# Reordering the row pairs of a hybrid decoder layer, splitting two embedding inputs at an earlier point, and scaling the last down-projection in PSUM

## The chip, the cores and the metric

The kernel runs on one core of a Trainium2 chip. The metric is device time in microseconds (us) of one execution; the median of several executions is compared. The engines are named as the profile names them: PE (TensorE, matmuls), PEld (its weight loads), DVE (VectorE), ACT (ScalarE), POOL (GpSimd) and SP (SyncE, which here issues nearly all DMA transfers). Each engine works through its own queue in order.

## The reference

One decoder layer over 1024 tokens with 1024 features, in float32. The parts that matter here, cut from the reference:

```python
h = x + mixed @ w_o                                # mixed: attention and convolution branches, normalised
a = rms_norm(h, ln_ffn_g) @ w_up                   # 1024 -> 2 x 2816
gate, up = split(a)
gate = causal_dwconv(gate, ffn_conv_w) + ffn_conv_b
h = h + (silu(gate) * up) @ w_down                 # 2816 -> 1024
h = h + sigmoid(rms_norm(h, ln_ple_g) @ w_pg) * (p_l @ w_pe)
```

`p_l` has 256 features per token: it is the embedding input, held transposed as `pT`.

## The kernel before

**Arithmetic.** Features lie on the 128 partitions and tokens along the free axis, in two halves of 512 (hf 0 and 1). Every float32 product is made of three matmuls: each operand is split into a high part (a cast to fp32r, `act.copy` or a POOL pass) and a low part (`dve.tensor_sub`, value minus high part), and `mm3` (L99 to L103) adds hi times hi (L101), hi times lo (L102) and lo times hi (L103). So each weight block and each activation costs, beside its load, one cast and one DVE subtraction before its matmuls.

**Row pairs (about 650 to 705 us).** The output projection `w_o` makes 8 row tiles per token half. Half 1 is done first in the loop at L944. Half 0 is done in four pairs (k, k+4) by `pair` (L1092), in between the first products of the up projection. For each row tile, `row` does 12 matmuls, and `row_rest` (L890) then does: DVE multiplies the PSUM tile by the token factor `rab` (L894), DVE adds the residual into `hm` (L896), SP writes `hm` to `hD`, ACT scales it into `y` (L899), ACT squares it (L903), DVE adds the square to `fssq` (L904). `forms_of` (L906) then makes the operands of a seven-product (Strassen-like) scheme out of four tiles of `y`: POOL makes t1, t2 and t4, DVE makes t3, and `keep_form` (L874) splits b22, t1, t3, t2 and t4 into a high part on ACT (L880) and a low part on DVE (L881). t3, t2 and t4 of pair k (the `late_` half of `forms_of`) are put one slot later, after the next pair's `row_rest`.

**What sets the order there.** This stage is written within a manual schedule (L1101): its loop goes over product slots n; each slot runs the matmuls of its pair or product, then the work that `behind(slot, delay, rank, function)` queued for it, sorted by rank, and `split(n + AHEAD)` puts the casts (`wbh`, L997) and subtractions (`wbl`, L998) of coming weight blocks in after the work of rank 0 and 1. POOL also makes sums of weight blocks (`wsum`, L984). In the lists below a tile named `bp` is a row tile in PSUM, `forms` is the tile that holds the split operands, `uv` is a copy of a product that ACT makes (L1058).

**Down projection (1110 to 1365 us).** The 22 gated activation tiles are taken in six groups of 3, 4, 4, 4, 4 and 3 (L1165). `act_parts` (L1134) loads and splits an activation (`acth`, `actl`). `down_group` (L1143) goes over 8 row tiles m: it loads and splits a block of `w_down` (`wraw`, `wh`, `wl`), does the matmuls of both token halves into PSUM tiles `ba`, and DVE adds them into `h` (L1154). In group 4 POOL then multiplies `h` by `rfb` and adds `hD` (L1160, L1163). In the last group DVE multiplies the PSUM tile by `rfb` into an SBUF tile `t` (L1157) and adds it to `h` (L1158).

**Embedding and gate (1358 to 1489 us).** `embed` (L1176) does the matmuls with `pT` and `w_pe`; two such tiles come before the gate projection, which needs all eight splits `fh`, `fl` (L1198, L1199) of the finished `h`. POOL adds six of the squares for the last norm (L1207).

**Order in this part.** Outside the manual schedule the framework orders each engine's queue by program order and readiness in its own model. `mark()` remembers the last instruction on every engine. A load with `after=` a mark gets a dependence on the mark's ACT instruction (L89 to L95), and the ACT cast in `weights` (L128) comes behind the mark in the queue. `pT` (two blocks of 512 KB) and `w_pe[0]` use the mark `last`. All `wraw` tiles share a ring of three buffers, and the DMAs are issued in order on SP.

Of the kernel before, what the change touches and what calls it, by code (L numbers as in the profile page):

```python
# [48 lines left out]
def _emit(nc, tc, d, out, tap=lambda *a: None):  # L49
# [824 lines left out]
    def keep_form(nm, k, y):  # L874
        i = FORMS.index(nm)
        where = i < 2, k
        if where not in forms_:
            forms_[where] = S([P, 2 if i < 2 else 5, 2, 512], F32R, f"forms{i < 2:d}{k}")
        hi, lo = (forms_[where][:, i if i < 2 else i - 2, z] for z in range(2))
        act.copy(hi, y)  # L880
        dve.tensor_sub(lo, y, f32(hi))  # L881
        form[nm][k] = hi, lo

# [6 lines left out]
    def row_rest(m, hf, ps):  # L890

        s = slice(hf * 512, (hf + 1) * 512)
        fs = fssq[:, s]
        dve.tensor_mul(ps, ps, rab[:, s])  # L894
        hm, g = S([P, 512], F32, "hm", 3), small["g_ffn"][:, m:m + 1]
        dve.tensor_add(hm, ps, hins[m, hf])  # L896
        nc.sync.dma_start(hD[m][:, s], hm)
# [1 line left out]
        act.activation(y, hm, AF.Copy, scale=g)  # L899
        if m == 0:  # L900
            act.square(fs, hm)
        else:
            act.square(ps, hm)  # L903
            dve.tensor_add(fs, ps, fs)  # L904

    def forms_of(k, late_=False):  # L906

        y11, y21, y12, y22 = (yf[m, hf] for hf in (1, 0) for m in (k, k + 4))

        def sub(nm, a, b, eng):  # L910
            z = yf[nm, k] = S([P, 512], F32, f"yt1{k}" if nm == "t1" else "yt", 1 if nm == "t1" else 3)
            eng.tensor_sub(z, a, b)
            return z
        if not late_:
            t1 = sub("t1", y12, y11, pool)
            keep_form("b22", k, y22)
            yf["t2", k] = sub("t2", y22, t1, pool)
            yf["t3", k] = sub("t3", y22, y12, dve)
            keep_form("t1", k, t1)
        else:  # L920
            z = sub("t4", y21, yf["t2", k], pool)
            for nm in ("t3", "t2"):
                keep_form(nm, k, yf[nm, k])
            keep_form("t4", k, z)
# [19 lines left out]
    for m in range(KC):  # L944
# [5 lines left out]
        row_rest(m, 1, ps)  # L950
        keep_form("b11" if m < 4 else "b21", m % 4, yf[m, 1])
# [140 lines left out]
    def pair(n, k):  # L1092
        tiles = [PS("bp", 4) for _ in range(2)]
        for m, ps in zip((k, k + 4), tiles):
            row(m, 0, ps)
# [89 lines left out]
    eh, el, wpe = [], [], {}  # L1185
    pT_h, pT_l = [], []
    for k in range(2):
        hi, lo = weights(d["pT"][k], 1024, tag="pT", bufs=2, after=last, by_act=True)
        pT_h.append(hi)
        pT_l.append(lo)  # L1190
# [147 lines left out]
```

## Time and profile before

| | us |
|---|---|
| median of 3 runs | 1489.8 |
| lowest and highest | 1489.61, 1490.05 |
| the profiled execution's own time | 1490.71 |
| its span in the trace | 1488.9 |
| PE busy within the span | 1433.8 |
| DVE busy | 990.5 |
| ACT busy | 584.2 |
| POOL busy | 492.6 |

The span runs from the first to the last instruction of the one execution that was profiled. PE is busy for 96% of it, so a saving is to be had only where PE stands idle or runs at the lower clock. In the trace's lists an idle time in square brackets stands just before an instruction, with the engine and line that released it. A duration of a matmul holds some overlap with the next; the distance between two starts is the true pace.

### The profile page before, as it was taken

What the parts mean: (1) busy time and instruction counts of PE and PEld (TensorE: products, weight loads), DVE (VectorE), ACT (ScalarE), POOL (GpSimd) and SP (SyncE); (2) the same over time, 40 slices, a digit from 0 to 9 for tenths busy, and PEclk for the clock granted to TensorE, in tenths of its full rate; (3) what the DMA queues carried; (4) which work ended last, traced back from release to release, by engine and by line L of the source; (5) the groups of instructions that cost most, each with busy time, mean ns of one, the idle gap of its engine ahead of it and who ended that gap; (6) DMA issues with size and microseconds to landing.
All of it is one profiled execution on the core that took longest, in us unless ns stands there. A gap on an engine that the chain in (4) does not pass through costs nothing.

```text
span 1488.9 us, 19441 instructions
## 1 busy us (share of the span) xinstructions
PE 1433.8 (96%) x7207; PEld 1168.9 (79%) x7207; DVE 990.5 (67%) x1588; ACT 584.2 (39%) x1190; POOL 492.6 (33%) x467
## 2 busy tenths in 40 slices
PE   7999999998999999986999999999999999997998
PEld 6787898996777777765888888888888888876887
DVE  7645566546778888777777777877774344469533
ACT  4110131237868889653323333233335112125211
POOL 3221242465445558245223333333310000474000
PEclk9999999999989999997999999999999999999999
DMA  6221214300000002241222222222235123341211
GB/s 250 82 71 56 75 58 155 104 1 1 1 1 1 1 1 86 93 149 63 72 74 68 71 85 85 86 86 85 78 114 184 57 106 114 103 160 69 71 43 43
DMA packets 48190, 115.50 MB, mean 78 GB/s; under 512 B 5472, under 2 KB 8160, under 8 KB 48096
## 3 DMA queue, kind: packets, MB, share of 16 engines
q1 hardware_dynamic: 48096, 114.26, 22.8%
q8 instruction: 57, 0.93, 0.3%
q14 instruction: 37, 0.30, 0.1%
HBM read 90.12 MB, written 24.12 MB: 77 GB/s over the span
## 4 chain that ended last, share of the span: by engine, by line
PE 55%; DVE 6%; ACT 2%; issue 2%; DMA 1%; POOL 1%; SPq 0%; ACTq 0%; DVEq 0%; POOLq 0%
PE uy L1018 12%; PE uz L1018 8%; PE ux L1018 8%; PE ba L102 6%; PE ba L103 6%; PE ba L101 6%; PE bv L753 2%; PE ba L719 1%; DVE forms L881 1%; ACT P L683 1%; DVE h L1158 1%; PE b L666 1%; DVE t L1157 1%; PE b L101 1%; PE b L667 0%
## 5 line engine op out<-in xcount | busy, mean ns | idle before, releaser
L1018 PE MATMUL uy<-forms,wbh 128*128 128x512 f32 x528 | 166.6, 397 | 0.0
L694 POOL TENSOR_SCALAR P<-P,sc,consts 128x64 f32<-128x64 f32 (+8 forms) x192 | 129.2, 683 | 103.6 <-DVE sc L692 98.0
L984 POOL TENSOR_TENSOR wsum<-wup,wup 128x512 f32<-128x512 f32 x44 | 71.8, 1632 | 234.5 <-DMA wup<-in_w_up 201.6
L102 PE MATMUL ba<-actl,wh 128*128 128x512 f32 x352 | 138.1, 394 | 1.7 <-DVE actl L1140 1.6
L103 PE MATMUL ba<-acth,wl 128*128 128x512 f32 x352 | 137.5, 393 | 0.0
L101 PE MATMUL ba<-acth,wh 128*128 128x512 f32 x352 | 137.2, 393 | 0.0
L998 DVE TENSOR_TENSOR wbl<-wsum,wbh 128x512 fp32r<-128x512 f32 x88 | 79.8, 907 | 66.3 <-ACT wbh L997 66.3
L1018 PE MATMUL uz<-forms,wbh 128*128 128x512 f32 x352 | 112.8, 401 | 8.3 <-DVE forms L881 3.3
L1018 PE MATMUL ux<-forms,wbh 128*128 128x512 f32 x352 | 111.9, 399 | 9.2 <-ACT uv L1058 9.2
L677 DVE TENSOR_REDUCE nmax<-b 128x1 f32<-128x64 f32 (+8 forms) x192 | 96.7, 539 | 36.0 <-PE b L669 35.3
L1018 PEld LDWEIGHTS uy<-forms,wbh 128*128 128x128 f32 x528 | 100.3, 190 | 23.4
L683 ACT ACTIVATE P<-b,nmax 128x64 f32<-128x64 f32 (+8 forms) x192 | 108.9, 576 | 19.8 <-DVE sc L692 12.1
L143 DVE TENSOR_TENSOR wl<-wraw,wh 128x1024 fp32r<-128x1024 f32 (+3 forms) x93 | 92.2, 995 | 31.7 <-ACT wh L140 14.4
L1018 PE MATMUL uy<-forms,wbl 128*128 128x512 f32 x264 | 104.7, 396 | 0.0
L1154 DVE TENSOR_TENSOR h<-h,ba 128x512 f32<-128x512 f32 x64 | 43.8, 686 | 89.9 <-PE ba L103 89.8
L719 PE MATMUL ba<-consts,P 128*128 128x128 f32 x592 | 91.2, 278 | 5.3 <-DVE pl L735 2.5
L142 POOL TENSOR_SCALAR wh<-wraw 128x1024 fp32r<-128x1024 f32 (+2 forms) x37 | 47.9, 1298 | 133.3 <-PE b L102 46.1
L140 ACT CAST wh<-wraw 128x512 fp32r<-128x512 f32 (+2 forms) x56 | 35.3, 647 | 143.5 <-PE ba L102 119.6
L1160 POOL TENSOR_TENSOR h<-h,rfb 128x1024 f32<-128x1024 f32 x8 | 22.4, 2795 | 205.9 <-DVE h L1154 203.5
L719 PEld LDWEIGHTS ba<-consts,P 128*128 128x128 f32 x592 | 68.9, 143 | 23.9 <-issue 7.7
L1018 PEld LDWEIGHTS ux<-forms,wbh 128*128 128x128 f32 x352 | 67.1, 191 | 25.4 <-ACT uv L1058 9.6
L1018 PEld LDWEIGHTS uz<-forms,wbh 128*128 128x128 f32 x352 | 67.4, 192 | 24.8 <-DVE forms L881 3.6
(306 smaller groups left out, 3854.3 us busy)
## 6 DMA issues: line engine op xcount, KB each, us to landing
wup<-in_w_up SPq DMA_DIRECT2D x88, 256.0 KB, 4.1
aD<-ua SPq DMA_DIRECT2D x22, 512.0 KB, 2.9
t<-aD SPq DMA_DIRECT2D x22, 512.0 KB, 4.5
wraw<-in_w_down SPq DMA_DIRECT2D x32, 256.0 KB, 5.6
wraw<-in_wA SPq DMA_DIRECT2D x13, 512.0 KB, 3.6
hinc<-in_xT SPq DMA_DIRECT2D x16, 256.0 KB, 3.4
h<-t SPq DMA_DIRECT2D x16, 256.0 KB, 2.4
hin<-h SPq DMA_DIRECT2D x16, 256.0 KB, 4.2
```

What stands on the lines that cost most here:

```text
L101: pe.matmul(ps, ah, bh, start=first, stop=False)
L102: pe.matmul(ps, ah, bl, start=False, stop=False)
L103: pe.matmul(ps, al, bh, start=False, stop=last)
L142: pool.tensor_scalar(hi, raw, 1.0, 1.0, op0=OP.mult, op1=OP.mult)
L143: dve.tensor_sub(lo, raw, f32(hi))
L677: dve.tensor_reduce(nmax[:, b:b + 1], ps[:, o:o + w], axis=AX.X, op=OP.max, negate=True)
L683: act.activation(pr[:, pc:pc + w], ps[:, o:o + w], AF.Exp, bias=nmax[:, b:b + 1], accum_out=den[:, b:b + 1])
L694: pool.tensor_scalar(pr[:, pc:pc + w], pr[:, pc:pc + w], sc[:, b:b + 1], gates[:, t, hd * 3 + b:hd * 3 + b + 1], op0=OP.mult, op1=OP.mult)
L719: pe.transpose(pt[0:k, r * P:(r + 1) * P], probs[u, r][:, pc:pc + k], ident)
L984: pool.tensor_tensor(t, a, b, op=op)
L998: dve.tensor_sub(lo, y, f32(hi))
L1018: pe.matmul(ps, a[:, k], b, start=new and k == n_mm == 0, stop=k == 3 and n_mm == 2, skip_group_check=not new)
```

## The change

There are three edits.

(A) **Row pairs.** `row_rest`, `forms_of` and `keep_form` are cut into single steps, and `pair_rest` puts them in a new order. Both rows of the pair get their multiply and residual add first. Then `pair_end(k - 1)` does the high and low parts of t3, t2 and t4 of the pair before. Then come the scalings, t1 and t2 on POOL, the high part of b22, the two squares, the high part of t1, the low parts and t3, and at the very end the two adds into `fssq` and t4 on POOL. The ring of `yt` goes from 3 to 5 buffers. In the loop at L944 each row's form is likewise split before its square is added.

(B) **Embedding inputs.** `last = mark()` moves from group 3 to group 4, after the activations of group 4 are split; the two blocks of `pT` are loaded and split right there, ahead of `down_group(4)`, and `w_pe[0]` ahead of `down_group(5)`. Before, both stood behind `down_group(5)` in the program.

(C) **Last down group.** The multiply by `rfb` writes back into the PSUM tile, and the add reads it from there. The SBUF tile `t` is no longer used there.

The core of the diff:

```diff
+    def pair_rest(k, tiles):
+        mm = (k, k + 4)
+        hms = [row_sum(m, 0, ps) for m, ps in zip(mm, tiles)]
+        pair_end(k - 1)
+        for m, hm in zip(mm, hms):
+            row_gain(m, 0, hm)
+        y11, y21, y12, y22 = (yf[m, hf] for hf in (1, 0) for m in mm)
+        sub("t1", k, y12, y11, pool)
+        sub("t2", k, y22, yf["t1", k], pool)
+        form_hi("b22", k, y22)
+        for m, hm, ps in zip(mm, hms, tiles):
+            row_square(m, 0, hm, ps)
+        form_hi("t1", k, yf["t1", k])
+        form_lo("b22", k, y22)
+        sub("t3", k, y22, y12, dve)
+        form_lo("t1", k, yf["t1", k])
+        for m, ps in zip(mm, tiles):
+            row_norm(m, 0, ps)
+        sub("t4", k, y21, yf["t2", k], pool)
+    def pair_end(k):
+        if k >= 0:
+            for fn in (form_hi, form_lo):
+                for nm in ("t3", "t2", "t4"):
+                    fn(nm, k, yf[nm, k])
...
-        for m, ps in zip((k, k + 4), tiles):
-            behind(n, 0, 0, lambda m=m, ps=ps: row_rest(m, 0, ps))
-        behind(n, 0, 1, lambda: forms_of(k))
-        behind(n, 1, 1, lambda: forms_of(k, True))
+        behind(n, 0, 1, lambda: pair_rest(k, tiles))
+        if k == 3:
+            behind(n, 1, 1, lambda: pair_end(k))
...
-                    t = S([P, 512], F32, "t2", 4)
-                    dve.tensor_mul(t, ps, rfb[:, s])
-                    dve.tensor_add(h[m][:, s], h[m][:, s], t)
+                    dve.tensor_mul(ps, ps, rfb[:, s])
+                    dve.tensor_add(h[m][:, s], ps, h[m][:, s])
...
-        if gi == len(GROUPS) - 3:
+        if gi == len(GROUPS) - 2:
             last = mark()
+            pT = [weights(d["pT"][k], 1024, tag="pT", bufs=2, after=last, by_act=True) for k in range(2)]
+        if gi == len(GROUPS) - 1:
+            wpe = {0: embed_weights(0)}
         down_group(gi, acts)
```

What stands in the engines' queues at three places, first in the kernel before, then in the changed one.

DVE at pair 1, from the multiply of its first row on (`rab` is the token factor, `forms<-yt` three times is the trio t3, t2, t4 of pair 0, `forms<-y_0` the low part of b22, `yt<-y_0,y_0` is t3):

```order
L894 TENSOR_TENSOR bp_7194<-bp_7194,rab_3041 128x512
L896 TENSOR_TENSOR hm_7230<-bp_7194,hin_7110 128x512
L904 TENSOR_TENSOR fssq_3042<-bp_7194,fssq_3042 128x512
L894 TENSOR_TENSOR bp_7195<-bp_7195,rab_3041 128x512
L896 TENSOR_TENSOR hm_7238<-bp_7195,hin_7112 128x512
L904 TENSOR_TENSOR fssq_3042<-bp_7195,fssq_3042 128x512
L881 TENSOR_TENSOR forms_1536_7177<-yt_7182,forms_1536_7177 128x512
L881 TENSOR_TENSOR forms_1536_7177<-yt_7180,forms_1536_7177 128x512
L881 TENSOR_TENSOR forms_1536_7177<-yt_7245,forms_1536_7177 128x512
L881 TENSOR_TENSOR forms_1554_7255<-y_0_1551_7241,forms_1554_7255 128x512
L912 TENSOR_TENSOR yt_7260<-y_0_1551_7241,y_0_1549_7233 128x512
L881 TENSOR_TENSOR forms_1554_7255<-yt_1553_7253,forms_1554_7255 128x512
```

```order
L883 TENSOR_TENSOR bp_7196<-bp_7196,rab_3041 128x512
L885 TENSOR_TENSOR hm_7232<-bp_7196,hin_7110 128x512
L883 TENSOR_TENSOR bp_7197<-bp_7197,rab_3041 128x512
L885 TENSOR_TENSOR hm_7236<-bp_7197,hin_7112 128x512
L915 TENSOR_TENSOR forms_1537_7176<-yt_7182,forms_1537_7176 128x512
L915 TENSOR_TENSOR forms_1537_7176<-yt_7174,forms_1537_7176 128x512
L915 TENSOR_TENSOR forms_1537_7176<-yt_7186,forms_1537_7176 128x512
L915 TENSOR_TENSOR forms_1555_7253<-y_0_1552_7247,forms_1555_7253 128x512
L903 TENSOR_TENSOR yt_7259<-y_0_1552_7247,y_0_1551_7245 128x512
L915 TENSOR_TENSOR forms_1555_7253<-yt_1553_7249,forms_1555_7253 128x512
L899 TENSOR_TENSOR fssq_3042<-bp_7196,fssq_3042 128x512
L899 TENSOR_TENSOR fssq_3042<-bp_7197,fssq_3042 128x512
```

The first `fssq` add stood between the two rows, the second ahead of the trio; now both rows' sums come together, the trio follows at once, and both `fssq` adds stand last.

ACT at the border of down groups 3 and 4 (the casts of `w_down` into `wh`, of the activations of group 4 into `acth`, of the embedding input into `pTh`):

```order
L140 CAST wh_11926<-wraw_11924 128x512
L140 CAST wh_11964<-wraw_11962 128x512
L140 CAST wh_12002<-wraw_12000 128x512
L1139 CAST acth_11908<-t_2495_11906 128x1024
L1139 CAST acth_11914<-t_2498_11912 128x1024
L1139 CAST acth_11920<-t_2501_11918 128x1024
L140 CAST wh_12040<-wraw_12038 128x512
```

```order
L1162 CAST acth_11908<-t_2495_11906 128x1024
L1162 CAST acth_11914<-t_2498_11912 128x1024
L1162 CAST acth_11920<-t_2501_11918 128x1024
L140 CAST pTh_11926<-wraw_11924 128x1024
L140 CAST pTh_11932<-wraw_11930 128x1024
L140 CAST wh_11938<-wraw_11936 128x512
```

Three casts of group 4's own weights stood ahead of the activations; now the first of them stands behind the activations and behind both casts of `pT`. On SP the loads of the first three of these weight blocks likewise stood in group 3, and now the first of them stands behind the two loads of `pT`.

DVE in the last down group, rows 4 and 5 of eight (`t` or `ba` times `rfb` is the multiply, `pTl` and `wpel` are the low parts of the embedding operands, `fl` those of the finished `h`):

```order
L1157 TENSOR_TENSOR t_2593_12390<-ba_12380,rfb_7081 128x512
L143 TENSOR_TENSOR pTl_12511<-wraw_12508,pTh_12510 128x1024
L1158 TENSOR_TENSOR h_2283_10766<-h_2283_10766,t_2593_12390 128x512
L1157 TENSOR_TENSOR t_2595_12403<-ba_12393,rfb_7081 128x512
L143 TENSOR_TENSOR wpel_12517<-wraw_12514,wpeh_12516 128x1024
L1158 TENSOR_TENSOR h_2283_10766<-h_2283_10766,t_2595_12403 128x512
L1157 TENSOR_TENSOR t_2600_12422<-ba_12412,rfb_7081 128x512
L143 TENSOR_TENSOR wl_12549<-wraw_12546,wh_12548 128x1024
L1158 TENSOR_TENSOR h_2284_10767<-h_2284_10767,t_2600_12422 128x512
L1157 TENSOR_TENSOR t_2602_12435<-ba_12425,rfb_7081 128x512
```

```order
L1179 TENSOR_TENSOR ba_12390<-ba_12390,rfb_7081 128x512
L143 TENSOR_TENSOR wl_12477<-wraw_12474,wh_12476 128x384
L1180 TENSOR_TENSOR h_2283_10766<-ba_12390,h_2283_10766 128x512
L1179 TENSOR_TENSOR ba_12402<-ba_12402,rfb_7081 128x512
L1223 SCALAR_TENSOR_TENSOR fl_2625_12557<-h_2282_10765,consts_61,fh_2624_12556 128x1024
L1180 TENSOR_TENSOR h_2283_10766<-ba_12402,h_2283_10766 128x512
L1179 TENSOR_TENSOR ba_12420<-ba_12420,rfb_7081 128x512
L143 TENSOR_TENSOR wl_12533<-wraw_12530,wh_12532 128x1024
L1180 TENSOR_TENSOR h_2284_10767<-ba_12420,h_2284_10767 128x512
L1179 TENSOR_TENSOR ba_12432<-ba_12432,rfb_7081 128x512
L1223 SCALAR_TENSOR_TENSOR fl_2628_12564<-h_2283_10766,consts_61,fh_2627_12563 128x1024
L1180 TENSOR_TENSOR h_2284_10767<-ba_12432,h_2284_10767 128x512
```

The low parts `pTl` and `wpel` are gone from this stretch, the adds read PSUM, and the `fl` subtractions have moved up between them.

## Rows read from the trace of the kernel before

**Rows 1.** Waits of PE: line, releaser, us in total, times, longest us.

```profile
PE ux L1018 <- ACT uv L1058: 9.2, 1, 9.2
PE b L101 <- DVE t L1157: 7.9, 2, 5.5
...
PE uz L1018 <- DVE forms L881: 3.3, 1, 3.3
PE uz L1018 <- ACT forms L880: 2.9, 1, 2.9
...
PE uz L1018 <- DVE uw L1026: 2.1, 1, 2.1
```

**Rows 2.** Busy time by stretch: PE, PEld, DVE, ACT, POOL, then clock, DMA.

```profile
650.00:705.00 55.00, 37.45 (x139) 29.36 (x138) 40.55 (x50) 23.21 (x42) 28.84 (x20) 0.78 0.21 67
...
1322.00:1365.00 43.00, 38.22 (x163) 29.76 (x161) 42.00 (x42) 21.09 (x25) 20.97 (x8) 1.00 0.38 132
```

**Rows 3.** Timeline of DVE in the row pairs.

```profile
658.87 2.66 DVE L881 TENSOR_TENSOR forms<-yt,forms 128x512 fp32r<-128x512 f32 x4
...
664.75 0.69 DVE L904 TENSOR_TENSOR fssq<-bp,fssq 128x512 f32<-128x512 f32 x1 [1.28 <-ACT bp L903]
...
672.82 1.75 DVE L998 TENSOR_TENSOR wbl<-wup,wbh 128x512 fp32r<-128x512 f32 x1
...
685.92 1.75 DVE L881 TENSOR_TENSOR forms<-yt,forms 128x512 fp32r<-128x512 f32 x1
```

**Rows 4.** Timeline of POOL in the same stretch.

```profile
670.63 1.72 POOL L912 TENSOR_TENSOR yt<-y,yt 128x512 f32<-128x512 f32 x1
```

**Rows 5.** Timelines of ACT in the row pairs and at the border of groups 3 and 4.

```profile
673.42 0.58 ACT L1058 COPY uv<-ux 128x512 f32<-128x512 f32 x1
...
1278.41 1.05 ACT L1139 CAST acth<-t 128x1024 fp32r<-128x1024 f32 x1 [2.54 <-PE ba L103]
1279.37 1.66 ACT L140 CAST wh<-wraw 128x512 fp32r<-128x512 f32 x3
```

**Rows 6.** Timeline of PE at the border of groups 3 and 4.

```profile
1278.91 0.40 PE L101 MATMUL ba<-acth,wh 128*128 128x512 f32 x1
```

**Rows 7.** DMA issues within 1278 to 1284 and 1322 to 1326: size, median us to landing.

```profile
t<-hD SPq DMA_DIRECT2D x3, 512.0 KB, 3.1
wraw<-in_w_down SPq DMA_DIRECT2D x2, 256.0 KB, 5.3
...
wraw<-in_pT SPq DMA_DIRECT2D x2, 512.0 KB, 6.0
```

**Rows 8.** Timeline of DVE in the last group and behind it.

```profile
1330.32 0.68 DVE L1157 TENSOR_TENSOR t<-ba,rfb 128x512 f32<-128x512 f32 x1
1331.10 2.10 DVE L1158 TENSOR_TENSOR h<-h,t 128x512 f32<-128x512 f32 x1
...
1345.53 1.21 DVE L143 TENSOR_TENSOR pTl<-wraw,pTh 128x1024 fp32r<-128x1024 f32 x1
...
1354.69 2.90 DVE L1158 TENSOR_TENSOR h<-h,t 128x512 f32<-128x512 f32 x1
...
1361.04 2.40 DVE L1158 TENSOR_TENSOR h<-h,t 128x512 f32<-128x512 f32 x2
...
1365.16 3.38 DVE L1199 SCALAR_TENSOR_TENSOR fl<-h,consts,fh 128x1024 fp32r<-128x1024 f32 x1
...
1371.47 7.06 DVE L1199 SCALAR_TENSOR_TENSOR fl<-h,consts,fh 128x1024 fp32r<-128x1024 f32 x4
```

**Rows 9.** Timeline of POOL in the last group.

```profile
1330.06 2.60 POOL L1163 TENSOR_TENSOR h<-h,t 128x1024 f32<-128x1024 f32 x1
```

**Rows 10.** Timeline of PE behind the last group.

```profile
1369.80 0.80 PE L101 MATMUL b<-pTh,wpeh 128*128 128x512 f32 x1 [5.53 <-DVE t L1157]
...
1374.78 0.40 PE L101 MATMUL ba<-fh,wh 128*128 128x512 f32 x1
...
1379.17 0.39 PE L102 MATMUL ba<-fl,wh 128*128 128x512 f32 x1
```

More of the change, by code (lines that the diff above doesn't have):

```diff
@@ L872, in _emit @@
     hD = [dram.tile([P, T], F32, name=f"hD_{m}") for m in range(KC)]
[L874 to L882, printed above, removed]
     def row(m, hf, ps):
@@ L888, in row, with row_sum, row_gain @@
             mm3(ps, wh[:, k], wl[:, k], oh[hf][:, k], ol[hf][:, k], k == 0, k == 3)
-    def row_rest(m, hf, ps):
+    def row_sum(m, hf, ps):
         s = slice(hf * 512, (hf + 1) * 512)
-        fs = fssq[:, s]
         dve.tensor_mul(ps, ps, rab[:, s])
-        hm, g = S([P, 512], F32, "hm", 3), small["g_ffn"][:, m:m + 1]
+        hm = S([P, 512], F32, "hm", 3)
         dve.tensor_add(hm, ps, hins[m, hf])
         nc.sync.dma_start(hD[m][:, s], hm)
+        return hm
+    def row_gain(m, hf, hm):
@@ L898, in row_rest @@
         y = yf[m, hf] = S([P, 512], F32, f"y{m}_{hf}")
[L899 to L903, printed above, removed]
-            dve.tensor_add(fs, ps, fs)
[L906 to L924, printed above, removed]
+        act.activation(y, hm, AF.Copy, scale=small["g_ffn"][:, m:m + 1])
@@ new lines, in row_square, with row_norm, sub, form_hi @@
+    def row_square(m, hf, hm, ps):
+        act.square(fssq[:, hf * 512:(hf + 1) * 512] if m == 0 else ps, hm)
+    def row_norm(m, hf, ps):
+        if m:
+            fs = fssq[:, hf * 512:(hf + 1) * 512]
+            dve.tensor_add(fs, ps, fs)
+    def sub(nm, k, a, b, eng):
+        z = yf[nm, k] = S([P, 512], F32, f"yt1{k}" if nm == "t1" else "yt", 1 if nm == "t1" else 5)
+        eng.tensor_sub(z, a, b)
+    def form_hi(nm, k, y):
+        i = FORMS.index(nm)
+        where = i < 2, k
+        if where not in forms_:
+            forms_[where] = S([P, 2 if i < 2 else 5, 2, 512], F32R, f"forms{i < 2:d}{k}")
+        form[nm][k] = tuple(forms_[where][:, i if i < 2 else i - 2, z] for z in range(2))
+        act.copy(form[nm][k][0], y)
@@ new lines, in form_lo @@
+    def form_lo(nm, k, y):
+        hi, lo = form[nm][k]
+        dve.tensor_sub(lo, y, f32(hi))
+    def pair_rest(k, tiles):
[17 more added lines that the diff above has]
+        sub("t4", k, y21, yf["t2", k], pool)
@@ L949, in _emit @@
         row(m, 1, ps)
-        row_rest(m, 1, ps)
-        keep_form("b11" if m < 4 else "b21", m % 4, yf[m, 1])
+        hm = row_sum(m, 1, ps)
+        row_gain(m, 1, hm)
+        row_square(m, 1, hm, ps)
+        nm = "b11" if m < 4 else "b21"
+        form_hi(nm, m % 4, yf[m, 1])
+        form_lo(nm, m % 4, yf[m, 1])
+        row_norm(m, 1, ps)
     rfb = S([P, T], F32, "rfb")
@@ L1163, in down_group, with embed_weights @@
                 pool.tensor_add(h[m], h[m], r)
+    def embed_weights(i):
+        return weights(d["w_pe"][i], 1024, tag="wpe", bufs=1, k=8, after=last, by_act=True)
     f = 0
@@ L1176, in embed @@
     def embed(m):
-        if m % 4 == 0:
-            wpe[m // 4] = weights(d["w_pe"][m // 4], 1024, tag="wpe", bufs=1, k=8, after=last, by_act=True)
+        if m == 4:
+            wpe[1] = embed_weights(1)
         wh, wl = (w[:, m % 4 * 2:m % 4 * 2 + 2] for w in wpe[m // 4])
@@ L1183, in embed @@
         return ps
[L1185 to L1190, printed above, removed]
+    eh, el = [], []
+    pT_h, pT_l = zip(*pT)
     emb = [embed(m) for m in range(2)]
```

3 lines of the change are left out of this document (2 added, 1 removed).

## The prediction

> **What bounds the kernel now.** I read the busy shares first: PE is busy for 1433.8 of 1488.9 us, so another engine's time counts only where PE waits for it. Next the list of PE's waits [rows 1], which gives the places that the change can reach. In the row pairs PE waits 9.2 us for the copy `uv`, 3.3 and 2.9 us for split operands, 2.1 us for `uw`. At the end it waits 7.9 us in two pieces for the multiplies of the last down group. Then the busy times by stretch [rows 2]: from 650 to 705 PE is busy for 37.45 of 55 us at a mean clock of 0.78, and DVE for 40.55; from 1322 to 1365 DVE is busy for 42.00 of 43 us and PE for 38.22. So DVE's queue is what PE waits for at both places. Third, the timelines [rows 3, 8], for what makes DVE slow there: a 512-wide subtraction out of SBUF steps at 0.6 us in one place (2.66 for four) and 1.75 in another, and the long one lies beside a POOL instruction of nearly the same length, 1.72 [rows 3, 4]. Last, the border of groups 3 and 4, where PE runs on without any idle time at 1278.91 [rows 6]: there edit B has nothing to gain, only something to lose.
>
> Two prices are needed throughout. **A collision:** a DVE instruction that reads two SBUF tiles while POOL runs takes about 1.7 instead of 0.6, a loss of 1.1 for each POOL instruction of that width. One that reads PSUM is not held: the multiply at 1330.32 took 0.68 inside a POOL instruction of 2.60, while the SBUF add behind it took 2.10 [rows 8, 9]. **The clock:** after the wait of 5.53 the 12 matmuls from 1369.80 to 1374.78 took 4.98 us, 0.415 each; the 19 from there to 1379.17 took 4.39, 0.231 each [rows 10]. [...]
>
> **Edit A, row pairs.** It removes, in each pair, two waits of DVE for a square of 1.28 us or a little more [rows 3], and moves the trio of low parts from ahead of the pair into it. From the end of the first row's `hm` of pair 2 (about 663.5) to the end of the next weight block's low part (672.82 + 1.75 = 674.57 [rows 3]) DVE spent 11 us. In the new order the same stretch holds a multiply and an add (1.3), seven steps with two SBUF inputs (trio, b22, t3, t1, the weight block) and two `fssq` adds from PSUM (1.2). POOL now does t1, t2, t4 and two weight sums back to back, so I let five of the seven steps pass at 1.7 and two at 0.6: 1.3 + 8.5 + 1.2 + 1.2 = 12.2, or 1.2 longer. But the pair begins earlier, since three of the four steps of the 2.66 row stand no longer ahead of it: 3 × 0.6 = 1.8. Net some 0.6 earlier for the product that waited 9.2 us. `uv` itself comes much earlier (it was copied at 673.42 [rows 5], behind high parts that now stand behind it), yet that wait is only handed on: the low part of the weight block is late next. For pair 3 the same balance is made once more: its step that PE waits for ended at 685.92 + 1.75 = 687.67 [rows 3], and following the new queue step by step puts it at 685.85, so 1.8 earlier; `uw` then gives 0.1. **Edit A: −1.9.** Bounds: with no collision at all the seven steps take 4.2 instead of 9.7, and the stretch 6.7, which is 4.3 less than the 11 and with the early start 6.1 less; then `uv` is the last, so **−6.0**. With all seven at 1.7 the stretch takes 14.4, 3.4 more, less 1.8 for the early start: 1.6 late, so I take **+1.6**. The chosen value lies near the upper bound, as the nearest rows (three steps in a row at 1.7 in the same stretch) do.
>
> **Edit B, the border of groups 3 and 4.** Before, three weight blocks of group 4 were loaded and cast within group 3, and PE ran on. In the new order SP reaches the first `pT` load only when ACT has cast the last activation of group 4. That cast starts at 1278.41 and takes 1.05, since it waits for a buffer that PE's last matmuls of group 3 free [rows 5]. So both `pT` loads, and behind them the first weight block of group 4, are issued at about 1279.5, with a 512 KB load of `hD` just ahead. Loads of 512 KB took 3.1 here and 6.0 in a denser place, 256 KB 5.3 [rows 7]. The first `pT` block thus lands at 1283 to 1284.4, the second some 1.4 later (an estimate: 6.0 − 3.1 is what two loads of that size add), the weight block half of that behind it, at 1285.3 to 1286.6. ACT casts `pT` (1.05 each by the row at 1278.41) and then the block (three in 1.66, 0.55 each [rows 5]); DVE follows with 1.21 for `pTl` [rows 8] and 0.68 for the block, which is ready at 1286.8 to 1289, middle 1288.3. The fourth matmul of group 4 needs it and ran at 1279.6 (three steps of 0.23 behind 1278.91). PE has nothing else in its queue: it stands for **8.7** us (7.2 to 9.5), and then comes the clock with 2.0: **+10.7** (7.2 if the clock costs nothing, 11.5 as upper end). Behind the wait, the 256 KB loads of group 4 come in time: a block of 24 matmuls gives 5.5 us for each.
>
> **Edits B and C, the end.** Three low parts leave the last group (`pTl` twice, `wpel`), 1.21 each: 3.6 us of DVE [rows 8]. The adds read PSUM and are no longer held: 2.10, 2.90 and 2.40 for two become 0.68 each, 1.42 + 2.22 + 1.04 = 4.7 less. But POOL's adds of squares are still there, and what they meet now are `fl` and `wl` subtractions: one `fl` took 3.38 beside a POOL instruction where four took 7.06, of which the free ones cost about 1.2 [rows 8]: 2.1 to 2.2 for each meeting, and there are two more of them, 4.2. Net 3.6 + 4.7 − 4.2 = 4.1, and a short replay of the new queue gives 4.8 for the last `fl`. PE needs that for the matmul at 1379.17 [rows 10]. The waits for the multiplies (7.9) go, yet a wait for `fl` comes in their place, and in pieces, since four `fl` end one behind another; some of it is paid at the lower clock, 0.4 to 2. **−4.4.** Bounds: all of the 7.9 and the clock's 2.0, **−9.9**; or 4.5 less a full 2.0 of clock, **−2.5**.
>
> [...]
>
> `wpel` now falls into group 4, where POOL multiplies and adds `h` nearly without a pause; it may hold that chain by 1.1 once. I cost it at nothing, as the next group's activations are wanted 30 us later.
>
> **Sum.** −1.9 + 10.7 − 4.4 = **+4.4** on the profiled execution's 1490.71, so 1495.1. That execution lies 0.9 above the median of the runs, so against 1489.8 I forecast **1494.2 us**. By the bounds alone the change lies between 7.2 − 6.0 − 9.9 = −8.7 and 11.5 + 1.6 − 2.5 = +10.6.
>
> **Rivals.**
> *Faster: POOL holds DVE less than I think, at both places.* Then edit A gives its −6.0 and the end its −9.9; with +10.7 the sum is −5.2, **1484.6**. It decides as soon as both together give more than 13.7, since a measurement tells about 0.2%, 3 us, from no change. For it: DVE's PSUM operations are not held, and the new order has more of these between. Against it: seven of the nine new steps in the row pairs have two SBUF inputs.
> *About the same: the border costs less,* because loads land in 3 us as those of `hD` did [rows 7] and PE's clock does not fall: 7.2 − 1.9 − 4.4 = +0.9, **1490.7**; or the end gives nearly all of its 9.9, 10.7 − 1.9 − 9 = −0.2, **1489.6**. Against the first: four loads share the queues within a microsecond, and the 6.0 of `pT` was measured in such a crowd.
> *Clearly slower: every collision is paid,* in the pairs (+1.6) and at `fl` (−2.5), with 11.5 at the border: +10.6, **1500.4**.
>
> **Chances.** Forecast (1492.8 to 1498) 0.45; about the same 0.25; faster 0.15; clearly slower 0.15. A gain of over 0.2% comes from the faster rival alone, 0.15; within 0.2% 0.25; slower 0.45 + 0.15 = 0.60. The range of 1486.5 to 1499.0 leaves out most of the faster rival and the far end of the last one, about 0.2 together.
>
> **What will show it.** In the new trace PE should wait once for 7 to 9 us at the first matmuls of group 4, on the cast `wh` or the low part `wl`, with `pT` loads issued about 1.1 us after the last `acth` cast begins, and matmuls 0.43 apart behind it. The wait for `uv` should be gone, and one of 7 to 9 us for the low part `wbl` at its place. Behind the last group there should be no wait for the multiplies, and waits for `fl` of some 3 to 5. If PE does not wait at group 4's start, the main term is wrong and the change is a gain of some 6 us; if the wait for `uv`'s product shrinks below 4 us, edit A was undervalued.

## The result, and the profile after

The change makes the kernel slower: 1497.4 us (median of 4 runs, 1496.8 to 1499.5) against 1489.9 before, a ratio of 1.0052 with a 95% interval of 1.0035 to 1.0069. The forecast of 1494.2 named the right sign, and the time lies within its range, 3 us above the forecast. The profiled execution of the changed kernel is the slowest of the four, 1499.52 with a span of 1497.7; it entered the row pairs 1.5 us later than that of the kernel before, and so stages are compared below by their own lengths.

PE's waits after (line, releaser, us in total, times, longest us), the list that answers to [rows 1]:

```profile
PE ba L101 <- ACT wh L140: 8.7, 1, 8.7
...
PE ux L1041 <- DVE wbl L1021: 5.4, 1, 5.4
...
PE ba L102 <- DVE actl L1163: 2.7, 1, 2.7
...
PE ba L165 <- POOL rfr L160: 2.1, 1, 2.1
PE ba L102 <- DVE fl L1223: 1.7, 1, 1.7
PE ux L1041 <- ACT uv L1081: 1.6, 1, 1.6
```

The first row is new and as long as forecast. The wait of 9.2 for `uv` is down to 1.6, and one of 5.4 for the weight block's low part stands behind it: the hand-over that the prediction described. The wait of 2.1 for `rfr`, at the entry of the row pairs, has no counterpart in the list of before. The 7.9 for the multiplies of the last group is gone, and small waits for `fl` have come. The wait for `actl`, the activations of the last group, is larger than the one of before, which was:

```profile
1327.77 0.50 PE L102 MATMUL ba<-actl,wh 128*128 128x512 f32 x1 [1.58 <-DVE actl L1140]
```

At the border of groups 3 and 4 (they are counted from 0), PE's timeline (answers to [rows 6]), then SP's, then the size of the weight block's load and the us from its issue to its landing, then ACT's:

```profile
1276.54 0.40 PE L103 MATMUL ba<-acth,wl 128*128 128x512 f32 x1
1285.63 0.80 PE L101 MATMUL ba<-acth,wh 128*128 128x512 f32 x1 [8.70 <-ACT wh L140]
...
1290.40 0.39 PE L102 MATMUL ba<-actl,wh 128*128 128x512 f32 x1
```

```profile
1277.35 0.81 SPq L91 DMA_DIRECT2D wraw<-in_pT  x2
1278.21 0.42 SPq L91 DMA_DIRECT2D wraw<-in_w_down  x1
```

```profile
wraw<-in_w_down SPq DMA_DIRECT2D x1, 256.0 KB, 6.4
```

```profile
1276.28 1.05 ACT L1162 CAST acth<-t 128x1024 fp32r<-128x1024 f32 x1 [24.75 <-PE ba L103]
1282.75 1.04 ACT L140 CAST pTh<-wraw 128x1024 fp32r<-128x1024 f32 x1 [5.43 <-DMA wraw<-in_pT]
1284.01 1.04 ACT L140 CAST pTh<-wraw 128x1024 fp32r<-128x1024 f32 x1 [0.21 <-DMA wraw<-in_pT]
1284.96 0.61 ACT L140 CAST wh<-wraw 128x512 fp32r<-128x512 f32 x1
```

Read from the bottom: PE's first matmul of group 4 follows the cast of its weight block at 1284.96, that cast the two of `pT`, the first of these its load, which SP issued at 1277.35, 1.07 us after ACT began the last activation cast. Each step is as forecast. The weight block itself landed 6.4 us behind its issue, at 1284.6, and was cast 0.3 us later; so nearly all of the wait is the queue of loads, and the casts of `pT` ahead of the block held it for 0.3 at most. Behind the wait the 11 matmuls from 1285.63 to 1290.40 took 4.77 us, at a granted clock of 0.50; at the pace of 0.231 [rows 10], where the clock was 1.00, they take 2.54, so the lower clock cost 2.2.

The lengths of the stages in the profiled executions, each from marks on ACT's and PE's timelines: the row pairs from the first scaling `y` of half 0 to the third copy `uv`; the up projection from there to the last `uv`; the down projection from there to the last matmul that reads `acth`; the end from there to the first norm-sum matmul (L156); the tail from there to the span's end.

| us | pairs | up | down | end | tail |
|---|---|---|---|---|---|
| before | 82.4 | 371.1 | 265.2 | 21.8 | 108.6 |
| changed | 79.4 | 370.1 | 280.2 | 15.1 | 111.6 |
| edit A alone | 80.1 | 370.4 | 265.7 | 21.3 | 112.0 |
| edit B alone | 82.3 | 371.1 | 277.7 | 20.7 | 111.6 |
| edit C alone | 82.6 | 371.1 | 265.2 | 17.9 | 108.4 |
| A and C | 79.8 | 370.4 | 265.9 | 16.4 | 110.1 |

Each row is one execution. In the runs beside the experiments single executions of the kernel before lay between 1483.2 and 1495.0, so a difference of one or two us between two rows shows little by itself.

Changed minus before: −3.0 − 1.0 + 15.0 − 6.7 + 3.0 = +7.3, the measured difference of the medians being 7.4. So two things were larger than forecast: the down projection (+15.0, not +10.7) and the tail (+3.0, forecast as part of the end); and the row pairs gave more.

### The profile page after: what moved, and what is told of

It is laid out like the page before. It is cut to its first block, busy times and chain, and to the rows that moved or that the text cites. A ratio compares the mean times of both kernels' runs of the same rounds, so it can differ in the third digit from the quotient of the medians.

```text
span 1497.7 us, 19417 instructions
## 1 busy us (share of the span) xinstructions
PE 1439.6 (96%) x7207; PEld 1172.2 (78%) x7207; DVE 1003.7 (67%) x1588; ACT 585.7 (39%) x1190; POOL 491.1 (33%) x467
## 4 chain that ended last, share of the span: by engine, by line
PE 47%; DVE 3%; issue 1%; DMA 1%; POOL 1%; ACT 0%; SPq 0%; DVEq 0%; POOLq 0%; ACTq 0%
PE uy L1041 12%; PE uz L1041 8%; PE ux L1041 7%; PE ba L101 6%; PE ba L102 6%; PE ba L103 6%; DVE wl L143 1%; DVE fl L1223 1%; DVE h L1180 1%; DVE ba L1179 1%; POOL h L1182 1%; DMA wraw<-in_pT 0%; PE b L101 0%; PE b L103 0%; PE b L102 0%
## 5 line engine op out<-in xcount | busy, mean ns | idle before, releaser
L143 DVE TENSOR_TENSOR wl<-wraw,wh 128x1024 fp32r<-128x1024 f32 (+3 forms) x93 | 100.8, 1089 | 31.8 <-ACT wh L140 15.6
L1041 PE MATMUL uz<-forms,wbh 128*128 128x512 f32 x352 | 112.0, 399 | 6.5 <-DVE forms L915 5.1
L101 PEld LDWEIGHTS ba<-acth,wh 128*128 128x128 f32 x352 | 67.0, 190 | 26.1 <-ACT wh L140 9.1
```

What stands on the lines that cost most here:

```text
L101: pe.matmul(ps, ah, bh, start=first, stop=False)
L143: dve.tensor_sub(lo, raw, f32(hi))
L1041: pe.matmul(ps, a[:, k], b, start=new and k == n_mm == 0, stop=k == 3 and n_mm == 2, skip_group_check=not new)
```

## The experiments

Each ratio is to runs of the kernel before that were taken beside the experiment (their medians lie between 1489.4 and 1490.7). Two kernels from different groups of runs are best compared by their ratios.

**One edit at a time.** Each of these is the kernel before with one edit, or with two; the diff is the part of the diff shown above.

*Edit A alone:*

> Edit A alone on the kernel before (row pairs reordered; embedding inputs and last down group as before). Theory 1 (edit A gains about 3 us, more than the 1.9 forecast, since in the changed kernel the stretch from the entry of the row pairs to the third product's copy uv became about 3 us shorter): 1486 to 1488, waits of PE in 650 to 705 some 13.5 us in sum. Theory 2 (the row pairs give the 1.9 or less, and what looked like more is scatter of single executions): 1488 to 1490.

Measured: 1489.1, ratio 0.9999 (0.9984 to 1.0014). *Edit B alone:*

> Edit B alone on the kernel before (both pT blocks split ahead of down group 4, w_pe ahead of group 5). Theory 1 (B stops PE at the start of group 4 for 8.7 us plus 2 us of clock, and delays the activations of the last group by 2 us more, and gives back 3 to 4 us at the end): 1497 to 1499.5. Theory 2 (the delay of the last group's activations comes from edit C or from the later start of GpSimd's chain alone and has no price of its own): 1495 to 1497.

Measured: 1503.4, ratio 1.0096 (1.0071 to 1.0120). *Edit C alone:*

> Edit C alone on the kernel before (scaling and add of the last down group out of PSUM). Theory 1 (adds no longer held by GpSimd, 4.7 us less of VectorE, about 4 us of which new meetings with fl and wl take back; PE waits at the end fall from 7.9 to some 6): 1487.5 to 1489.5. Theory 2 (nothing is taken back, the gain is 4 us): 1485 to 1487. [...]

Measured: 1486.0, ratio 0.9976 (0.9961 to 0.9990), in the range of theory 2. *Edits A and C:*

> Edits A and C without B. Theory 1 (the two add up, since they lie 600 us apart): 1489.8 minus the gains of the two single kernels, 1484.5 to 1487. Theory 2 (B's earlier pT is what makes C worth something, A gives under 2): 1487.5 to 1489.5. In no case a wait at the start of group 4.

Measured: 1483.3, ratio 0.9963 (0.9948 to 0.9978), a lower time than either theory had.

So the loss is B's alone: 14 us by itself, more than any theory had, and 13 on top of A and C (1.0052 against 0.9963). C gains 3.4, and A gains nothing by itself; with C it adds 2.7 to C's gain, but the intervals of these two kernels overlap. In the table A alone has pairs and up projection that are 2.9 us shorter, and a tail that is 3.4 longer. PE's timeline of edit A alone, in front of and behind the norm's sums, and then the same place in the kernel before:

```profile
1373.32 0.50 PE L102 MATMUL ba<-fl,wh 128*128 128x512 f32 x1 [2.54 <-DVE fl L1222]
...
1374.52 0.80 PE L102 MATMUL ba<-fl,wh 128*128 128x512 f32 x1 [0.23 <-DVE fl L1222]
...
1376.85 3.57 PE L156 MATMUL ba<-consts,pssq 128*128 128x1 f32 x16
1380.29 0.77 PE L101 MATMUL ba<-fh,wh 128*128 128x512 f32 x1
```

```profile
1380.31 1.84 PE L156 MATMUL ba<-consts,pssq 128*128 128x1 f32 x16
1382.01 0.49 PE L101 MATMUL ba<-fh,wh 128*128 128x512 f32 x1
```

The 16 records of the norm's one-column matmuls took 3.57 us instead of 1.84, at the lower clock (the full matmuls from 1375.11 to 1376.39 start 0.43 apart, as in the changed kernel at a granted clock of 0.50), just behind PE's waits for `fl` (2.54 and 0.23 us). Before, PE waited for the multiplies earlier, paid the low clock on the embedding's matmuls [rows 10] and had the full clock again by then (granted 1.00 from 1380.30 to 1382.00). So in this execution what A saved in the pairs was lost here. Edit C alone has no wait for `fl` in that place and keeps its tail of 108.4.

**Which part of B costs what.** The changed kernel with `w_pe` back in its old place of the program (the mark that its load waits for stays the later one):

```diff
-        if gi == len(GROUPS) - 1:
-            wpe = {0: embed_weights(0)}
...
-        if m == 4:
-            wpe[1] = embed_weights(1)
+        if m % 4 == 0:
+            wpe[m // 4] = embed_weights(m // 4)
```

> The changed kernel with w_pe loaded and split where it was before; pT still ahead of group 4. Theory 1 (the 3.6 us that PE waits for the last group's activations come from w_pe's load and low part within group 4): these waits fall to 1.6 or less, as in the kernel before, 1494 to 1496. Theory 2 (they come from GpSimd's chain in group 4, which starts 8.7 us behind PE's first matmul there instead of 6.5, since VectorE does low parts of two more blocks first): the waits stay at 3 to 4 us, 1497 to 1499.

Measured: 1494.8, ratio 1.0039 (1.0022 to 1.0055). The waits for the last group's activations, in the changed kernel and then here:

```profile
1334.04 0.49 PE L101 MATMUL ba<-acth,wh 128*128 128x512 f32 x1 [0.97 <-ACT acth L1162]
1337.20 0.50 PE L102 MATMUL ba<-actl,wh 128*128 128x512 f32 x1 [2.66 <-DVE actl L1163]
...
1338.44 0.63 PE L102 MATMUL ba<-actl,wh 128*128 128x512 f32 x1
...
1341.42 0.39 PE L101 MATMUL ba<-acth,wh 128*128 128x512 f32 x1
```

```profile
1330.00 0.73 PE L101 MATMUL ba<-acth,wh 128*128 128x512 f32 x2 [0.36 <-ACT acth L1162]
1332.24 0.50 PE L102 MATMUL ba<-actl,wh 128*128 128x512 f32 x1 [1.04 <-DVE actl L1163]
```

They fall from 3.63 to 1.40 us, and the time to the 1494 to 1496 of theory 1. The two ratios, 1.0052 and 1.0039, have intervals that overlap, so the times alone don't show the 2 us between them; the waits do. In the traces of the four kernels with `w_pe` in group 4 they come to 2.7 to 3.6 us in sum (B alone and the kernel below without GpSimd's adds 2.7; the one with `pT` in buffers of its own 3.1, though it has no wait at the border), in those of the ten others to 1.4 to 1.7, with one exception, 2.5 in the last one below. DVE and POOL in group 4 of the changed kernel show how:

```profile
1305.55 3.39 DVE L143 TENSOR_TENSOR wpel<-wraw,wpeh 128x1024 fp32r<-128x1024 f32 x1 [0.17 <-ACT wpeh L140]
1308.87 2.89 DVE L143 TENSOR_TENSOR wl<-wraw,wh 128x512 fp32r<-128x512 f32 x1
1311.68 1.27 DVE L1177 TENSOR_TENSOR h<-h,ba 128x512 f32<-128x512 f32 x2
```

```profile
1313.10 2.72 POOL L1182 TENSOR_TENSOR h<-h,rfb 128x1024 f32<-128x1024 f32 x1 [1.89 <-DVE h L1177]
```

`wpel` and the low part behind it, 1.2 and 0.7 us when free, are both held by POOL's steps; so DVE adds the product into `h` late, and POOL stands for 1.89 us, where its pauses in the kernel without `w_pe` there are 0.26 to 0.40. With `w_pe` in group 4 the loads of the last two activations are issued 43.0 us behind group 4's first matmul, without it 41.9, in the kernel before 39.4: they wait for buffers that POOL's adds of `hD` free. So `w_pe` accounts for 1.1 us of that delay; the other 2.5 come with the border (and cost nothing by themselves: PE waits 1.40 with them), since POOL's chain starts 8.7 to 9.0 us behind group 4's first matmul instead of 6.5. In the changed kernel the longer wait has the lower clock behind it as well (1338.44 to 1341.42: seven matmuls in 2.98 us, 0.43 each, at a granted clock of 0.50); behind the longest ones of the kernel without GpSimd's adds (1.34) and of the one with `pT` in buffers of its own (1.67) the matmuls stay 0.23 apart.

**What the border's wait is.** The changed kernel, with `pT`'s raw blocks in buffers of their own, loaded in the program ahead of group 3 (SP issues them at 1203.22 and 1204.42, some 70 us before group 4 begins); casts and low parts stay where the change put them:

```diff
+        if gi == len(GROUPS) - 3:
+            soon = mark()
+            praw = [S([P, 1024], F32, "praw", 2) for _ in range(2)]
+            for k in range(2):
+                load(praw[k], d["pT"][k], soon)
...
-            pT = [weights(d["pT"][k], 1024, tag="pT", bufs=2, after=last, by_act=True) for k in range(2)]
+            pT = [weights(d["pT"][k], 1024, tag="pT", bufs=2, raw=praw[k], after=last, by_act=True) for k in range(2)]
```

> The changed kernel with one thing else: pT's raw blocks get buffers of their own and are loaded within group 3; their casts and low parts stay ahead of down group 4 as in the changed kernel. Theory 1 (the wait of 8.7 us is the load behind the last activation cast, in the ring that it shares with the weight blocks): the wait at the start of group 4 goes to under 1 us, and the time to 1481 to 1486. Theory 2 (casts and low parts of pT ahead of group 4's first block cost ACT 2.1 and VectorE 2.4 us on PE's path anyway): a wait of 2 to 4.5 us stays, 1487 to 1491.

Measured: 1485.4, ratio 0.9964 (0.9948 to 0.9981). PE does not wait there at all. ACT's timeline at the border:

```profile
1274.21 1.05 ACT L1162 CAST acth<-t 128x1024 fp32r<-128x1024 f32 x1 [2.55 <-PE ba L103]
1275.17 1.99 ACT L140 CAST pTh<-praw 128x1024 fp32r<-128x1024 f32 x2
1277.07 0.61 ACT L140 CAST wh<-wraw 128x512 fp32r<-128x512 f32 x1
```

The two `pT` casts follow the activation's at once. They still stand ahead of a cast of a weight block, but of the fourth one: with the ring free, the first three of group 4 were loaded and cast within group 3 again, as before the change. So the price was the load in the shared ring and in SP's queue. Theory 2, the casts on PE's path, falls with it, and the 0.3 us between landing and cast at the border of the changed kernel says the same.

**Another place for B.** A and C, with the embedding inputs split within group 3:

```diff
+            if gi == 3 and m in (1, 3):
+                pT.append(weights(d["pT"][len(pT)], 1024, tag="pT", bufs=2, by_act=True))
+            if gi == 3 and m == 5:
+                wpe[0] = embed_weights(0)
...
-            pT = [weights(d["pT"][k], 1024, tag="pT", bufs=2, after=last, by_act=True) for k in range(2)]
-        if gi == len(GROUPS) - 1:
-            wpe = {0: embed_weights(0)}
```

> Edits A and C, and the embedding inputs split within down group 3 (pT behind rows 1 and 3, w_pe behind row 5), each behind weight blocks of its group and without a dependence on a mark. Theory 1 (the price of edit B is its place, at a border where the load has to wait for the last activation cast; in group 3 VectorE is half idle and GpSimd does nothing): no wait of PE at the borders, 3.6 us less of VectorE in the last group than with A and C alone (1483.3), so 1479 to 1481.5. Theory 2 (any split of 512 KB blocks in the ring of three raw buffers makes the weight blocks late): a wait of 3 to 9 us in group 3 or 4, 1486 to 1492.

Measured: 1482.2, ratio 0.9951 (0.9935 to 0.9968), a little above theory 1's range. No wait at a border (the queues run ahead of PE: DVE makes `pT`'s low parts at 1211.6 and 1222.7, while PE is still in group 2). But the 3.6 us less of VectorE in the last group gave no more than 1 to 2 us, within the scatter, over A and C alone (0.9963). The stage "end" is 16.4 us in both. The next two experiments show what took the 3.6 us back.

**GpSimd's adds of squares.** The changed kernel without POOL's six adds into `pssq`:

```diff
-            (pool if k < KC - 1 else dve).tensor_add(pssq, pssq, sq)
+            if k == KC - 1:
+                dve.tensor_add(pssq, pssq, sq)
```

> The changed kernel without GpSimd's six adds of squares into pssq (they are left out, so the last norm lacks six of its eight terms). Theory 1 (each of them holds one fl or wl subtraction, 8.3 us in sum over the last group): the last fl is ready about 5 us or more before PE needs it, no waits for fl and no low clock in front of the norm's sums, 3.1 + 3 us less: 1490.5 to 1492.5. Theory 2 (VectorE is not what the end waits for): 1495.5 to 1498.

Measured: 1487.9, ratio 0.9991 (0.9975 to 1.0007), 9.4 us less than the changed kernel: more than theory 1 had. Two of the last `fl` subtractions on DVE in the changed kernel, and beside them an add from PSUM that lies within POOL's add from 1357.23 to 1360.41; then one of the kernel without the adds:

```profile
1358.06 0.68 DVE L1180 TENSOR_TENSOR h<-ba,h 128x512 f32<-128x512 f32 x1
...
1367.95 2.99 DVE L1223 SCALAR_TENSOR_TENSOR fl<-h,consts,fh 128x1024 fp32r<-128x1024 f32 x1
...
1378.43 2.45 DVE L1223 SCALAR_TENSOR_TENSOR fl<-h,consts,fh 128x1024 fp32r<-128x1024 f32 x1
```

```profile
1365.94 1.27 DVE L1223 SCALAR_TENSOR_TENSOR fl<-h,consts,fh 128x1024 fp32r<-128x1024 f32 x1
```

The four `fl` that met POOL's adds took 2.45 to 2.99, and each takes 1.27 or 1.28 here. The end goes from 15.1 to 11.3 with no wait of PE in it, the tail from 111.6 to 108.4, and the down projection, which the theories did not count, from 280.2 to 278.4. The held subtractions read two SBUF tiles; the add `h` beside them, which reads one tile in PSUM and one in SBUF, stayed at 0.68.

**Who should add the squares.** The kernel with the inputs split in group 3, with the squares of tiles 4 to 6 added by VectorE:

```diff
-            (pool if k < KC - 1 else dve).tensor_add(pssq, pssq, sq)
+            (pool if k < 4 else dve).tensor_add(pssq, pssq, sq)
```

> The kernel with the embedding inputs split in group 3, with one thing else: the squares of tiles 4, 5 and 6 are added into pssq by VectorE (1.2 us each) and no longer by GpSimd, whose three adds held fl subtractions of 2.97, 2.86 and 2.42 us, 1.28 each when free. Theory 1 (a GpSimd add costs VectorE about what the add costs VectorE itself, 1.1 to 1.7 us against 1.2): the last fl comes within 1.5 us of where it was, time 1480.5 to 1483.5. Theory 2 (VectorE's chain only grows): 1484 to 1487.

Measured: **1479.5**, ratio 0.9930 (0.9911 to 0.9950), better than both theories and than the kernels before and after the change. Its interval overlaps that of the kernel that it was made from (0.9935 to 0.9968), so the 3 us between these two are not shown by the times alone; the traces show an end that is 3.3 us shorter. DVE's last steps there, and in the kernel that it was made from:

```profile
1357.37 1.27 DVE L1225 SCALAR_TENSOR_TENSOR fl<-h,consts,fh 128x1024 fp32r<-128x1024 f32 x1
...
1359.17 1.21 DVE L1233 TENSOR_TENSOR pssq<-pssq,t 128x1024 f32<-128x1024 f32 x1
1360.30 1.28 DVE L1225 SCALAR_TENSOR_TENSOR fl<-h,consts,fh 128x1024 fp32r<-128x1024 f32 x1
```

```profile
1360.23 2.42 DVE L1225 SCALAR_TENSOR_TENSOR fl<-h,consts,fh 128x1024 fp32r<-128x1024 f32 x1
```

An `fl` and an add cost DVE 2.4 us in its own queue, as much as the shortest of the three `fl` held by POOL's adds (2.42 to 2.97): by that alone some 1 us is gained. The larger part of the gain (end 13.1 instead of 16.4) is two low parts of later weight blocks, 2.35 us, that the framework now puts behind the last `fl`, where they had stood ahead of it. The end is 1.8 us above the 11.3 without waits.

**Squares as chunks on PE.** From the kernel with the inputs split in group 3:

```diff
-            (pool if k < KC - 1 else dve).tensor_add(pssq, pssq, sq)
+            if k < 6:
+                pool.tensor_add(pssq, pssq, sq)
+            else:
+                late_sq.append(sq)
...
-                    rp = rstd(pssq, NT, D, "rp")
+                    rp = rstd([pssq] + late_sq, NT, D, "rp")
```

> The kernel with the embedding inputs split in group 3, with one thing else: the squares of the last two tiles are not added into pssq (one GpSimd add beside an fl, and VectorE's own add of 1.2 us) but go into the norm's sums on PE as chunks of their own, 16 more one-column matmuls of 0.11 us. Theory 1 (the end waits for VectorE's chain): the waits of 1.6 and 0.4 us before the norm's sums go, and the low clock in them with it, less 1.8 for the matmuls: 1479 to 1481.5. Theory 2 (that chain is no longer the bound, PE's own work is): 1483 to 1485.

Measured: 1487.2, ratio 0.9988 (0.9975 to 1.0001), a loss where theory 1 had a gain, and above theory 2's range. The waits for `fl` did shrink (end 14.6, not 16.4), but the tail grew from 110.3 to 115.5. PE's timeline of the norm's sums:

```profile
1371.28 0.28 PE L156 MATMUL ba<-consts,pssq 128*128 128x1 f32 x2
1371.42 0.58 PE L156 MATMUL ba<-consts,t 128*128 128x1 f32 x4
...
1375.44 0.96 PE L156 MATMUL ba<-consts,t 128*128 128x1 f32 x4
...
1377.55 0.77 PE L101 MATMUL ba<-fh,wh 128*128 128x512 f32 x1
```

There are now three operands for each of eight token blocks, and each matmul stands as two records (16 for eight blocks and one operand before), so the string has 48 records and grew by 32, not by the 16 that the expectation counted. It lasts 6.27 us, from 1371.28 to 1377.55. And within the string, with no wait in it, the pace falls from 0.11 to 0.21 each at 1375.44, and the full matmuls from 1378.12 on start 0.43 apart, as in the changed kernel at a granted clock of 0.50. So theory 1 was right about the waits, and its price for the sums was wrong twice.

**The trio's place in the row pairs.** From the kernel with the inputs split in group 3, `pair_end(k - 1)` moved behind the pair's own forms:

```diff
         hms = [row_sum(m, 0, ps) for m, ps in zip(mm, tiles)]
-        pair_end(k - 1)
...
         form_lo("t1", k, yf["t1", k])
+        pair_end(k - 1)
```

> The kernel with the embedding inputs split in group 3, with one thing else: in each row pair the parts of t3, t2 and t4 of the pair before stand behind the pair's own b22, t3 and t1, not ahead of them. Theory 1 (what VectorE loses in a pair is set by the number of GpSimd's instructions, five at about 1.1 us each, whichever of its steps they meet): PE's wait for the weight block's low part stays at 4 to 5 us, time within 2 us of 1482.2. Theory 2 (it is the trio's place that costs, 4.8 us for three steps instead of 1.9): that wait falls by about 2.9, to 1479 to 1480.5. Theory 3 (VectorE now stands idle for the scaling of the second row, 1 us or more per pair): 1484 to 1487.

Measured: 1486.5, ratio 0.9979 (0.9967 to 0.9991). The pairs became 3.3 us longer than in the kernel that it was made from (82.6 instead of 79.3), PE's wait for the low part stayed (4.07, from 4.28), the one for `forms` fell from 5.08 to 2.04, and two new ones came, 1.48 for `uv` and 3.63 for another low part. DVE in pair 2 there, and in the changed kernel, whose order of the pairs is the same as in the kernel that it was made from:

```profile
663.55 1.24 DVE L915 TENSOR_TENSOR forms<-y,forms 128x512 fp32r<-128x512 f32 x1 [1.52 <-ACT forms L911]
...
665.32 5.72 DVE L915 TENSOR_TENSOR forms<-yt,forms 128x512 fp32r<-128x512 f32 x4
```

```profile
664.93 4.81 DVE L915 TENSOR_TENSOR forms<-yt,forms 128x512 fp32r<-128x512 f32 x3
669.66 1.76 DVE L915 TENSOR_TENSOR forms<-y,forms 128x512 fp32r<-128x512 f32 x1
671.35 1.75 DVE L903 TENSOR_TENSOR yt<-y,y 128x512 f32<-128x512 f32 x1
673.02 0.68 DVE L915 TENSOR_TENSOR forms<-yt,forms 128x512 fp32r<-128x512 f32 x1
...
674.94 0.68 DVE L1021 TENSOR_TENSOR wbl<-wup,wbh 128x512 fp32r<-128x512 f32 x1
```

Without the trio in front, DVE stands idle until ACT has the high part, 1.5 us in each of pairs 1 and 2 and 2.2 in pair 3: theory 3, with theory 1 right about the wait that it named. In the order of edit A the trio of the pair before fills that gap. *With both of the last two changes:*

> Both of the above together. If the two places are apart, the sum of their differences to the kernel with the inputs split in group 3 (1482.2): by theory 1 of both 1479 to 1482.

Measured: 1490.9, ratio 1.0006 (0.9995 to 1.0017), far from the 1479 to 1482: the two changes are losses, and as losses they add up.

## Why the prediction was right or wrong

- **Border of groups 3 and 4: right in mechanism and size.** The wait was 8.70 (forecast 8.7), the clock 2.2 (forecast 2.0, though 12 matmuls at 0.415 instead of 0.231 [rows 10] make 2.2). The loads and the casts came in the order that the queues gave. That the wait is met to the tenth is luck: the forecast reckoned up to the low part `wl` at the fourth matmul, while PE's first matmul waited for the high part `wh`, and the first one that reads `wl` ran 1.4 us behind it.
- **`w_pe` in group 4: the term that was wrong.** The prediction costed it at nothing, "as the next group's activations are wanted 30 us later". But their loads wait for buffers that POOL's chain frees, that chain was nearly without a pause, and PE waited 1.58 us for these activations already before the change: there was no slack. Of the two steps of the argument the first failed by size (the chain stood for 1.89 us, not 1.1) and the second altogether. The waits went from 1.58 to 3.63 us, and the low clock behind them cost some 1.6 more in the profiled execution (the nine matmuls from 1337.77 to 1341.42 take 2.1 at 0.231 each). Without `w_pe` there they are 1.40, and the ratio is 1.0039 instead of 1.0052, 2 us.
- **Edit A: right mechanism, too small.** Forecast −1.9, measured −3.0 in the pairs and −1.0 in the up projection. In the pairs the steps went as written: five of seven at 1.6 to 1.76 us, two at 0.68, `uv` early, and a wait for the weight block's low part in its place (forecast 7 to 9; in fact 5.4, with 1.6 for `uv` still ahead of it, 7.0 together). The value of −1.9 lies in the middle of its bounds, −6.0 and +1.6, not near the upper one as the prediction says. What it left out is the clock: the mean granted clock went from 0.78 [rows 2] to 0.84. That PE's shorter waits brought the clock back sooner fits this, but no run shows it apart:

```profile
650.00:705.00 55.00, 41.46 (x162) 32.29 (x163) 48.46 (x55) 23.67 (x42) 31.82 (x23) 0.84 0.21 72
```

  Where the 0.6 to 1.4 in the up projection comes from, which every kernel with edit A shows, stays open. PE has no wait there: before and after the change it runs the same 1597 matmuls at a granted clock of 1.00, 0.2325 us apart before and 0.2318 after.
- **The end: the sum right, the terms less so.** Forecast −4.4, measured −6.7 + 3.0 = −3.7. The adds from PSUM were not held (0.68 or 0.69), and GpSimd's adds met `fl` and `wl` in their place, as forecast; four `fl` were held, by 1.2 to 1.7 us each and not by 2.1. The low clock, taken at 0.4 to 2, was 3.0 (granted 0.50 from 1386.13 to 1389.70): about 1.7 of it on the 16 records of the norm's sums (the L156 row of the changed kernel below is to be held against the 1.84 of before) and 1.4 on the seven full matmuls behind them.

```profile
1385.00 0.51 PE L102 MATMUL ba<-fl,wh 128*128 128x512 f32 x1 [1.73 <-DVE fl L1223]
...
1386.13 3.57 PE L156 MATMUL ba<-consts,pssq 128*128 128x1 f32 x16 [0.41 <-DVE pssq L1231]
```

- **PSUM against SBUF.** Edit C alone gained 3.4 us (0.9976), the size that theory 2 had, though its "nothing is taken back" is not what the trace shows: in the last group a `wl` of 2.92 and two `fl` of 2.20 and 2.90 were held there, as theory 1 said. Its adds out of PSUM took 0.68 or 0.69, as forecast, and free subtractions within SBUF 0.67 [rows 3].
- **The rivals.** The faster one ("POOL holds DVE less") fell: held subtractions took 1.6 to 1.76 in the pairs and 2.4 to 3.0 at the end. That the border might cost less fell too. Of the slower rival two parts did not come (edit A's +1.6 and an end of only −2.5), and what made the kernel slower than the forecast was in none of them.
- **The sum.** By stages the terms were −4.0 for edit A (forecast −1.9), +15.0 for the border with the last group's activations (+10.7) and −3.7 for the end (−4.4). So the time lies within its range in part because A's gain, larger than forecast, made up for half of what was missing for B.

## What to carry to other kernels

A split that is moved earlier brings its load with it: look at which buffers the load takes, at what stands behind it in the queue, and at the last wait ahead of it, since here PE, which ran without a pause at that border between loops, stood for 8.7 us, while the loads took 7.3 from the first `pT` issue to the landing of the weight block. An add that was handed to GpSimd to spare VectorE cost VectorE here about as much as doing it, where VectorE's instructions beside it read two SBUF tiles (a hold of 1.2 to 1.7 us against an add of 1.2); with three of them moved back the kernel had its lowest time, two thirds of that gain being the order of the queue that came with it. Slack that a term rests on is to be read from the waits: PE waited for these activations before anything was moved. And a saving that left TensorE waiting in small pieces just ahead of short matmuls was paid back in clock: with edit A alone the 16 records of the norm's sums took 3.57 us instead of 1.84, behind waits of 2.54 and 0.23.

## What the runs showed of the hardware that was not expected

In the kernel with the squares as chunks the pace fell within a string of one-column matmuls in which PE did not wait: from 1371.28 on the records stood 0.11 us apart, from 1375.44 on 0.21 apart, and the full-width matmuls behind them 0.43 apart, the pace that the changed kernel had at a granted clock of 0.50. PE's last wait ahead of the string was 0.44 us long, at 1370.72. Sixteen such records at the full clock were followed by the full clock where PE had not waited since the embedding's matmuls or earlier (before: 1.84 us for the 16, at a granted clock of 1.00, which held to 1390 at least; the kernel without GpSimd's adds: 1.84 as well, and the full matmuls from 1377.85 on 0.23 apart), and soon by the lower one where it had waited just ahead of them (the squares of tiles 4 to 6 added by VectorE: waits of 0.82 and 0.40 us, 1.95 for the 16, and the full matmuls from 1367.27 to 1370.25 0.43 apart). How much the string and how much the waits count, no run separates.
